# A hybrid mixer block on one core: bias rows replicated with the 128 rows outermost, result tiles reserved when a projection begins, and another weight order

## The chip, the core and the metric

The kernel runs on one core of a Trainium2 chip. The core has five engines that work at the same time: TensorE (PE, matrix products; its weight loads are PEld), VectorE (DVE), ScalarE (ACT), GpSimd (POOL) and SyncE (SP, which here only issues DMAs). Each engine runs its own instructions strictly in the order in which they were written and waits on semaphores for the others. Sixteen DMA engines move data between the chip's memory and the on-chip buffer. The metric is the device time of one execution in microseconds (us); lower is better.

## What is computed

One transformer-like block on 512 tokens of width 1024. The normalised input is multiplied by a wide matrix `w_in`, the product is split over four mixers, their outputs are multiplied by `w_out`, added to the input and normalised:

```python
h = _rmsnorm(x, norm_g[l])
p_fox, p_ssm, p_nsa, p_mem = _split(h @ w_in[l], [FOX_COLS, SSM_COLS, NSA_COLS, MEM_COLS])
mem_kv = _rmsnorm(mem, mem_norm_g[l]) @ w_mem_kv[l]
o = jnp.concatenate([
    _fox_mixer(p_fox, fox_f_bias[l]),
    _ssd_mixer(p_ssm, conv_w[l], conv_b[l], dt_bias[l], a_log[l], d_skip[l], norm_g[l]),
    _nsa_mixer(p_nsa, cmp_pe[l], cmp_w1[l], cmp_w2[l], rel_bias_table),
    _mem_mixer(p_mem, mem_kv),
], axis=-1)
x = x + o @ w_out[l]
return _rmsnorm(x, final_norm_g)
```

Fox is causal attention with forget gates (8 heads); ssd, called ssm in the kernel, a state-space scan in 4 chunks of 128 tokens; nsa compressed, selected and window attention (8 heads); mem attention to 256 memory tokens (4 heads). The nsa mixer adds a bias to each score that depends only on the distance of query and key and on the head (`rel_table[_t5_bucket(dist)]`).

## The kernel before

**Weights.** All matrices lie in memory as tiles of 128 x 1024 float32 (512 KB), one after the other in the order of the table `ORDER`. A tile takes three steps, in this order: SP loads it into one of three `raw` buffers; ACT rounds it to a short format (`wh`, function `split`); POOL subtracts to get the rest (`wl`). The matrix product is then taken as three products (`wh` with `hh`, `wh` with `hl`, `wl` with `hh`, where `hh` and `hl` are the same two parts of the input), so that a column block of 128 outputs (a "projection", `tile_a`) is 24 matmuls into a PSUM tile `pj`. There are three `wh` and three `wl` buffers too: a tile can be split when the third tile before it has been multiplied, and a `raw` buffer is free for the next load when POOL has made its `wl`. In this text T1, T2, ... are the tiles of `ORDER` from the eighth entry on, where the projections begin. `fq`, `fk`, `fg` are queries, keys and gates of fox; `kc` and `vc` keys and values for nsa's compression; `mv`, `mk`, `mq` belong to mem; `xb`, `z` to ssm; `wo` to the output product (`po`).

**Order of the work.** A planner in the kernel (`Clock`, `Sched`, `Pipe`) runs while the program is written. It keeps an estimated time for each engine and decides, step by step, whether the next matmuls are a step of one of the mixers (`fox`, `mem`, `nsa`, `ssm`, the compression `cmp`, the ssm preparation `pre`; the first `ACTIVE` entries of `PIPES`) or a piece of three matmuls of the next projection. `DF, DM, DN, DS` are how many steps each mixer may have in flight, `RF, RM, RN, RS` how many buffer slots are kept free for its later steps. `gs` and `bs` are counters of two pools of tiles; `TAKES` says what a projection takes of them. On the chip nothing of the planner is left: the engines run the written order.

A step of fox (`s1` to `s4`) is: scores on PE (`pS`), the mask and the negative row minimum on DVE (`pF`, `nm`), exponentials on ACT, reciprocal on DVE (`rs`), scaling, transposes on PE (`pT`), a copy out of PSUM (`pt`, on DVE or ACT), the product with the values on PE (`pO`). When `fq` is done, ACT and DVE make the tiles `L` (4 instructions) and then ACT makes `M` (4 instructions). `pre` builds the tiles `bd` and `cgs` on DVE. The compression multiplies `kc` and `vc`, spread out in `xst`, by weights `w1` (4 x 512 KB, loaded by SP when it begins): the matmuls `pcm`.

**The bias rows.** `rel_bias` computes 8 rows (one per head) of 656 biases (`prv`) and writes them to memory as `rv`. `spread(j)` then copies, from memory to memory, the rows of two heads (j and j + 4) 128 times each into `rows[j]`, 2 x 128 x 656 float32 (656 KB). `bias_tile(j)` later reads `rows[j]` back, with each of the 128 partitions shifted by one element. Spreads 0 and 1 are issued on SP right behind `rv`; spreads 2 and 3 when nsa begins its first and second pair of heads. SP is also the queue of every weight load.

**The end.** The last weight tiles are `wo1`, the output product of ssm. The four chunks c of ssm run between other `po` matmuls: `pR`, `pG`, `pX`, `pB` on PE; on DVE `m` (two times pR + mask), `xdt`, `xde`, two times `m` x `pG`; exponentials on ACT; then `pst` and `pY` on PE, where `pY` needs `m`, and from chunk 1 on `ce` and the state `prev` of the chunk before, which DVE makes.

Of the kernel before, what the change touches and what calls it, by code (L numbers as in the profile page):

```python
# [21 lines left out]
RVW = 656  # L22
WARM = 12
NL = 3
DF, DM, DN, DS = 5, 3, 5, 3
BACKLOG = 3000
RAW, RING = 3, 3
PIPES = "fox", "cmp", "mem", "pre", "ssm", "nsa"
LAST = 1
ACTIVE = 4  # L30

RF, RM, RN, RS = 4, 3, 2, 7

SOON, LATER, WIDE = 500, 1500, 3500

TAKES = {"fq": (2, 1), "fk": (2, 1), "fg": (1, 0), "nq": (2, 0), "ng": (1, 0), "z": (1, 0), "mq": (2, 0), "mg": (1, 0),
         "mk": (1, 0), "ks": (0, 4), "kw": (0, 4), "kc": (1, 1), "vc": (1, 1), "xb": (2, 0), "mv": (4, 0),
         "rel": (2, 0), "wo0": (5, 4), "wo1": (5, 4), "wo2": (5, 4), "wo3": (5, 4)}
# [1 line left out]
FOX, SSM, NSA, MEM = 0, 2056, 3600, 5416  # L40

ORDER = (
# [10 lines left out]
)  # L53
# [304 lines left out]
def block_kernel(ctx, tc, I, out):  # L358
    nc = tc.nc
    clock = Clock()  # L360
    V, A, P, T, Q = (Engine(e, n, clock) for e, n in (
        (nc.vector, "DVE"), (nc.scalar, "ACT"), (nc.gpsimd, "POOL"), (nc.tensor, "PE"), (nc.sync, "SP")))
# [6 lines left out]
    gs, bs = Store(NG), Store(NB)  # L369
# [5 lines left out]
    def B4(name, shape, dt=FT):  # L375
        bs.take()
        return sb.tile(shape, dt, name=name, tag="b4", bufs=NB)
# [10 lines left out]
    def PS(name):  # L388
        t = ps.tile([128, 512], FT, name=name, tag="ps", bufs=8)
        clock.bank(t.name)  # L390
        return t
# [13 lines left out]
    def unring(name, t):  # L405
        left = rings[name]
        left[0] += 1
        left[1].append(max(clock.used[t.name].values()))
        left[1].sort()
# [31 lines left out]
    def get(key):  # L441
        i = state["next"]
        assert ORDER[i] == key, (ORDER[i], key)
        state["next"] += 1
        split(i + 1)
        ahead()
        return wh.pop(i), wl.pop(i)

    def done(pair):
        unring("wh", pair[0])  # L450
        unring("wl", pair[1])
# [65 lines left out]
    def three(out_, a, b, first, last, n):  # L517
        pairs = ((a[0], b[0]), (a[0], b[1]), (a[1], b[0]))
        for i, (x, y) in enumerate(pairs):
            T.matmul(out_, x, y, start=first and i == 0, stop=last and i == 2)  # L520
# [123 lines left out]
    def memory(whole=False):  # L644

        while side and side[0]:
            if next(side[0], 1):
                side[0] = None
            if not whole:
                break  # L650
# [10 lines left out]
    def tile_a(key, sink, h=None, width=512):  # L661
        h_, l_ = get(key)
        if h:
            memory(True)
        hi, lo = h if h else (hh, hl)
        yield max(clock.ready([h_, l_, *hi, *lo]), clock.free_banks(1))
        p = PS("pj")
        for k in range(KT):
            cs = slice(k * 128, (k + 1) * 128)
            three(p[:, :width], (h_[:, cs], l_[:, cs]), (hi[k], lo[k]), k == 0, k == KT - 1, width)  # L670
            if k < KT - 1:
                yield 0.0
        done((h_, l_))
        sink(p[:, :width], key)
        if key == KEYS_A[-1]:
            gs.drop(16)
# [166 lines left out]
    def out_last(t):  # L843
# [16 lines left out]

    adders = {
        "fq": lambda k: tile_a(k, s_fq),
        "fk": lambda k: tile_a(k, s_fk),
        "fg": lambda k: tile_a(k, s_gate),
        "nq": lambda k: tile_a(k, s_q),
        "ng": lambda k: tile_a(k, s_gate),
# [160 lines left out]
    rows = [dr.tile([2, 128, RVW], FT, name=f"rows{j}") for j in range(4)]  # L1027
# [16 lines left out]
    def rel_bias():  # L1044
        sbv = G("rvs", FT, 512), G("rvt", FT, 512)
        for i in range(2):
            p = PS("prv")
            cs = slice(i * 328, (i + 1) * 328)
            T.matmul(p[:8, :328], tb, oneh[:, cs], start=True, stop=True)
            A.activation(sbv[i][:8, :328], p[:8, :328], AF.Copy, scale=-1.0)  # L1050
            Q.dma_start(out=rv[:, cs], in_=sbv[i][:8, :328])
        yield 0
        gs.drop(2)
        bs.drop()
        spread(0)
        spread(1)

    def spread(j):
        src = rv[j:j + 1, :]
        Q.dma_start(out=rows[j], in_=bass.AP(tensor=src.tensor, offset=src.offset, ap=[[4 * RVW, 2], [0, 128], [1, RVW]]))  # L1060

    def bias_tile(j):
        t = B4("bt", [128, 2, BTW])
# [8 lines left out]
    def alloc_kx():  # L1072
        if kx:
            return
        kx.extend([B4(f"k{x}{a}", [128, 1056], FR) for a in range(2)] for x in "hl")
        for a in range(2):
            P.memset(kx[1][a][64 - 64 * a:128 - 64 * a].bitcast(FT), 0.0)
            V.memset(kx[0][a][:, 512:544].bitcast(FT), 0.0)
            x = slice(64 * a, 64 * a + 64)
            V.memset(kx[1][a][x, 512:544].bitcast(FT), 0.0)  # L1080
# [83 lines left out]
    def nsa():  # L1164
        st, bts = {}, {}

        def s1(s):
            j, b, a = s
            if b == 0 and a == 0:
                if j == 0:  # L1170
                    bts[0] = bias_tile(0)
                if j < 3:
                    bts[j + 1] = bias_tile(j + 1)
                if j < 2:
                    spread(j + 2)
# [169 lines left out]
    pre = []  # L1345
# [304 lines left out]
    made = {"fox": fox, "cmp": compress, "mem": mem, "nsa": nsa, "ssm": ssm, "pre": prep}  # L1650
    bg.run([made[n]() for n in PIPES])
    while bg.todo:
# [113 lines left out]
```

## Time and profile before

| | us |
|---|---|
| median of 3 runs | 570.41 (570.08 to 571.86) |
| the profiled execution, its own time | 571.07 |
| its span, first to last instruction | 568.9 |
| PE busy in the span | 540.7 (95%) |
| PEld, DVE, ACT, POOL busy | 449.8, 332.1, 317.6, 236.4 |
| mean granted clock of PE | 0.982 of full speed |
| moved by DMA | 59.01 MB, mean 104 GB/s |

PE is busy for 95% of the span, so time goes down only where PE waits, or where it runs below full speed. The other engines are busy for about half of the time. Matmuls overlap in this profile: a matmul's own length is longer than the distance to the next one's start, and the distance is what counts for the sum.

### The profile page before, as it was taken

To read this page: it belongs to the slowest core of one execution; us is meant where nothing else is said; L and a number is where in the kernel's file an instruction comes from. 1 tells how busy PE (TensorE), PEld (TensorE's weight loads), DVE (VectorE), ACT (ScalarE), POOL (GpSimd) and SP (SyncE) were. 2 spreads that over 40 slices of the span, in tenths; PEclk is the share of its full clock that TensorE was granted. 3 is DMA by queue.
4 is the path that set the end of the run, shared out by engine and by line. 5 is a ranking of instruction groups with operands and counts; after the bars stand their busy time and mean duration, and the time that the engine had idled before them with its cause. 6 is when DMAs were issued, how large, how long until landed. Compare 5 with 4: busy or idle time off the path is not lost.

```text
span 568.9 us, 8824 instructions
## 1 busy us (share of the span) xinstructions
PE 540.7 (95%) x3237; PEld 449.8 (79%) x3237; DVE 332.1 (58%) x869; ACT 317.6 (56%) x712; POOL 236.4 (42%) x159
## 2 busy tenths in 40 slices
PE   8999999999199999999999999999999999999695
PEld 5898778777188798888888888888888888888584
DVE  2666866565057535564466546765656655666653
ACT  5756547694126655566566656656656655544333
POOL 3594514231078553334232231551533235568432
PEclk9999999999689999999999999999999999999898
DMA  7772232202723332432123211622221222123013
GB/s 286 299 264 92 103 92 75 74 15 83 240 101 99 135 112 93 138 117 75 58 103 112 74 46 67 261 74 75 74 75 38 75 74 75 38 74 112 0 39 111
DMA packets 18736, 59.01 MB, mean 104 GB/s; under 512 B 2132, under 2 KB 2404, under 8 KB 18693
## 3 DMA queue, kind: packets, MB, share of 16 engines
q1 hardware_dynamic: 18548, 58.19, 29.7%
q8 instruction: 25, 0.41, 0.3%
q10 hardware_dynamic: 144, 0.26, 0.1%
q14 instruction: 19, 0.15, 0.1%
HBM read 55.80 MB, written 4.81 MB: 107 GB/s over the span
## 4 chain that ended last, share of the span: by engine, by line
PE 79%; DVE 7%; ACT 6%; DMA 6%; issue 1%; POOL 0%; SPq 0%; POOLq 0%; DVEq 0%; ACTq 0%
PE pj L231 35%; PE po L231 15%; PE pO L231 6%; PE pb L231 6%; PE pT L231 5%; DMA raw<-in_wst 5%; PE pS L231 4%; PE pmv L231 2%; PE pW L231 1%; ACT pF L231 1%; PE pY L231 1%; DMA xt<-in_xT 1%; DVE Rl L231 1%; ACT M L231 1%; ACT wh L231 1%
## 5 line engine op out<-in xcount | busy, mean ns | idle before, releaser
L231 POOL TENSOR_TENSOR wl<-raw,wh 128x1024 fp32r<-128x1024 f32 (+1 forms) x72 | 172.2, 2396 | 282.1 <-ACT wh L231 268.6
L231 PE MATMUL pj<-hh,wh 128*128 128x512 f32 x352 | 143.4, 407 | 0.0
L231 PE MATMUL pj<-hh,wl 128*128 128x512 f32 x352 | 137.8, 392 | 0.0
L231 PE MATMUL pj<-hl,wh 128*128 128x512 f32 x352 | 137.6, 391 | 0.0
L231 ACT ACTIVATE wh<-raw 128x1024 fp32r<-128x1024 f32 (+1 forms) x72 | 74.8, 1041 | 27.8 <-DMA raw<-in_wst 23.1
L231 PEld LDWEIGHTS pj<-hh,wl 128*128 128x128 f32 x352 | 66.2, 188 | 14.8
L231 PEld LDWEIGHTS pj<-hh,wh 128*128 128x128 f32 x352 | 66.3, 188 | 13.6 <-issue 2.2
L231 PEld LDWEIGHTS pj<-hl,wh 128*128 128x128 f32 x352 | 66.5, 189 | 10.8
L231 ACT ACTIVATE pN<-pN,nm 128x128 f32<-128x128 f32 (+7 forms) x96 | 45.3, 473 | 22.9 <-DVE nm L231 22.1
L231 PE MATMUL po<-wh,oh 128*128 128x512 f32 x96 | 39.2, 409 | 0.0
L231 PE MATMUL po<-wh,ol 128*128 128x512 f32 x96 | 37.6, 392 | 0.0
L231 PE MATMUL po<-wl,oh 128*128 128x512 f32 x96 | 37.6, 391 | 0.0
L231 ACT ACTIVATE pN<-pN,rs 128x128 f32<-128x128 f32 (+3 forms) x32 | 18.0, 564 | 28.4 <-DVE rs L231 28.4
L231 DVE SCALAR_TENSOR_TENSOR sg<-sg,pj 128x512 f32<-128x512 f32 x16 | 11.0, 688 | 31.9 <-ACT sg L231 31.9
L231 DVE SCALAR_TENSOR_TENSOR xs<-cb,cwh,xs 128x512 f32<-128x512 f32 x24 | 18.0, 752 | 17.7 <-ACT xs L231 17.1
L231 DVE TENSOR_SCALAR rs<-sm 128x3 f32<-128x3 f32 x32 | 11.3, 354 | 28.7 <-ACT pN L231 28.7
L231 ACT ACTIVATE pF<-pF,nm 128x128 f32<-128x128 f32 (+3 forms) x32 | 17.7, 553 | 17.3 <-DVE nm L231 17.3
L231 DVE CUSTOM_DVE_ANT_0 pN<-pS,bt 128x128 f32<-128x128 f32 (+4 forms) x72 | 20.9, 328 | 10.2 <-PE pS L231 10.0
L231 DVE TENSOR_TENSOR acc<-acc,po 128x512 f32<-128x512 f32 (+1 forms) x33 | 21.1, 664 | 8.8 <-PE po L231 8.8
L231 PE MATMUL pO<-pt,fv 128*64 128x128 f32 x160 | 13.3, 302 | 12.0 <-ACT pt L231 12.0
L231 DVE COPY pt<-pT 128x512 f32<-128x512 f32 (+1 forms) x32 | 19.6, 618 | 7.2 <-PE pT L231 7.0
L231 PE MATMUL pT<-cst,pN 128*128 128x128 f32 x160 | 23.1, 275 | 0.0
(273 smaller groups left out, 1114.5 us busy)
## 6 DMA issues: line engine op xcount, KB each, us to landing
raw<-in_wst SPq DMA_DIRECT2D x74, 512.0 KB, 3.3
rows<-rv SPq DMA_DIRECT2D x4, 656.0 KB
bt<-rows SPq DMA_DIRECT2D x4, 528.0 KB, 4.2
xt<-in_xT SPq DMA_DIRECT2D x8, 256.0 KB, 7.0
xn<-in_xn SPq DMA_DIRECT2D x4, 512.0 KB
w<-in_w SPq DMA_DIRECT2D x4, 512.0 KB
acc<-in_xn SPq DMA_DIRECT2D x4, 512.0 KB
out<-acc SPq DMA_DIRECT2D x7, 256.0 KB, 2.2
```

Of the source, the lines that this page charges most:

```text
L231: return f(*a, **k)
```

## The change

Four things. (1) `spread` lists the dimensions of the copy in another order: the 128 repetitions outermost and the two heads inside them, for source and destination alike; the same bytes go to the same places. (2) `tile_a` takes the slots of its result from `gs` and `bs` when it begins and gives them back just before the result is written, so that the planner doesn't hand them to a mixer meanwhile; for `ks` and `kw` the key tiles `kx` are allocated (and partly zeroed) when the projection begins. (3) Numbers of the planner: depths, kept slots, the order of `PIPES`. (4) The order of the weights.

```diff
-DF, DM, DN, DS = 5, 3, 5, 3
+DF, DM, DN, DS = 6, 4, 3, 3
-PIPES = "fox", "cmp", "mem", "pre", "ssm", "nsa"
+PIPES = "fox", "pre", "cmp", "mem", "ssm", "nsa"
-RF, RM, RN, RS = 4, 3, 2, 7
+RF, RM, RN, RS = 4, 3, 2, 8
 ORDER = (
-    ("bv", 0), ("bv", 1), ("bv", 2), ("bv", 3), ("bc", 0), ("bc", 1), ("bc", 2), ("fq", 0),
-    ("fk", 0), ("fk", 2), ("vc", 0), ("fq", 3), ("fg", 0), ("fk", 1), ("fq", 1), ("fq", 2),
+    ("bv", 0), ("bv", 1), ("bv", 2), ("bv", 3), ("bc", 0), ("bc", 1), ("bc", 2), ("fq", 1),
+    ("fq", 0), ("fk", 0), ("fq", 2), ("fg", 0), ("mq", 0), ("fq", 3), ("fk", 1), ("fk", 2),
...
         hi, lo = h if h else (hh, hl)
+        if key[0] in ("ks", "kw"):
+            alloc_kx()
+        g, b = TAKES[key[0]]
+        b = 0 if key[0] in ("ks", "kw") else b
+        gs.take(g)
+        bs.take(b)
         yield max(clock.ready([h_, l_, *hi, *lo]), clock.free_banks(1))
...
         done((h_, l_))
+        gs.drop(g)
+        bs.drop(b)
         sink(p[:, :width], key)
...
     def spread(j):
         src = rv[j:j + 1, :]
-        Q.dma_start(out=rows[j], in_=bass.AP(tensor=src.tensor, offset=src.offset, ap=[[4 * RVW, 2], [0, 128], [1, RVW]]))
+        Q.dma_start(out=rows[j].rearrange("a p w -> p a w"),
+                    in_=bass.AP(tensor=src.tensor, offset=src.offset, ap=[[0, 128], [4 * RVW, 2], [1, RVW]]))
```

What this does to the order of the instructions is seen at three places.

SP's queue around the first two spreads (`rows_487`, `rows_488`), as a difference; `raw` is a weight tile, `xst` the spread-out `kc` or `vc`, `w_1502` to `w_1507` are `w1`:

```order
 L231 DMA w_496<-in_w 128x128
-L231 DMA raw<-in_wst 128x1024 x4
+L231 DMA raw<-in_wst 128x1024 x11
 L231 DMA xst<-kv 64x511
 L231 DMA xst<-kv 64x512
-L231 DMA raw<-in_wst 128x1024 x6
 L231 DMA rv<-rvs 8x328
 L231 DMA rv<-rvt 8x328
-L231 DMA rows_487<-rv 256x1x656
-L231 DMA rows_488<-rv 256x1x656
+L231 DMA rows_487<-rv 128x2x656
+L231 DMA rows_488<-rv 128x2x656
 L231 DMA raw<-in_wst 128x1024
```

Behind it both have `xst` (of `kc`); then before two weight loads and the change one, and then the four loads of `w1`. Before, ten weight tiles after `w_496` are ahead of the spreads, so the load right behind them is that of T15; in the change eleven are ahead, and the load behind them is that of T16.

ACT's queue at the first softmax of fox (`pF`), before:

```order
L231 ACTIVATE Rk<-pj 64x512 x2
L231 ACTIVATE wh<-raw 128x1024
L231 CAST ar<-pa 64x128
L231 COPY kv<-pj 128x512
L231 ACTIVATE wh<-raw 128x1024
L231 ACTIVATE pF,sm<-pF,nm 128x128 x2
```

and in the change:

```order
L231 ACTIVATE Rk<-pj 64x512 x2
L231 CAST ar<-pa 64x128
L231 ACTIVATE wh<-raw 128x1024
L231 ACTIVATE L<-pj 64x512 x2
L231 ACTIVATE M<-pj 64x512
L231 ACTIVATE M<-cst 64x512
L231 ACTIVATE M<-pj 64x512
L231 ACTIVATE M<-cst 64x512
L231 ACTIVATE wh<-raw 128x1024
L231 ACTIVATE pF,sm<-pF,nm 128x128 x2
```

The `L` and `M` of one more query block (`fq` 2) now stand ahead of the first exponentials. DVE's part of `L` stands between `cgs` and the first `pF` there.

DVE's queue at the last two ssm chunks, before:

```order
L231 TENSOR_TENSOR ol<-of,oh 128x512
L231 TENSOR_TENSOR m<-pR,umask 128x512 x2
L231 TENSOR_TENSOR xdt<-pX,dtv 128x512
L231 TENSOR_TENSOR xde<-xdt,dte 128x512
L231 TENSOR_TENSOR m<-m,pG 128x512 x2
L231 TENSOR_TENSOR acc<-acc,po 128x512 x2
L231 TENSOR_TENSOR m<-pR,umask 128x512 x2
```

and in the change:

```order
L231 TENSOR_TENSOR ol<-of,oh 128x512
L231 TENSOR_TENSOR acc<-acc,po 128x512 x2
L231 TENSOR_TENSOR m<-pR,umask 128x512 x2
L231 TENSOR_TENSOR xdt<-pX,dtv 128x512
L231 TENSOR_TENSOR xde<-xdt,dte 128x512
L231 TENSOR_TENSOR m<-m,pG 128x512 x2
L231 TENSOR_TENSOR m<-pR,umask 128x512 x2
```

The two additions of `po` to `acc` moved ahead of chunk 2. On PE the nine `po` matmuls that stood between chunk 2's `pR` to `pB` and chunk 3's `pR` now stand ahead of chunk 2's; and nine `po` of the last product stand right behind `pY`, ahead of chunk 2's `pn`.

## Rows read from the trace of the kernel before

**Rows 1.** The page: the span; PE's busy tenths in 40 slices.

```profile
span 568.9 us, 8824 instructions
...
PE   8999999999199999999999999999999999999695
```

**Rows 2.** PE's timeline: matmuls that PE waited for longest (start, length; idle before).

```profile
78.67 0.44 PE L231 MATMUL pT<-cst,pF 128*128 128x128 f32 x2 [1.42 <-ACT pF L231]
...
155.78 2.82 PE L231 MATMUL pO<-pt,fv 128*64 128x128 f32 x22 [11.97 <-ACT pt L231]
...
532.62 0.44 PE L231 MATMUL pY<-m,xdt 128*64 128x128 f32 x4 [2.93 <-DVE m L231]
535.28 0.70 PE L231 MATMUL pY<-ce,prev 128*64 128x128 f32 x4 [2.21 <-DVE prev L231]
```

**Rows 3.** ACT's timeline at the end of PE's longest wait.

```profile
154.41 1.06 ACT L231 ACTIVATE wh<-raw 128x1024 fp32r<-128x1024 f32 x1 [15.11 <-DMA raw<-in_wst]
155.37 0.84 ACT L231 COPY pt<-pT 128x256 f32<-128x256 f32 x2
```

**Rows 4.** Three pieces of the chain that ended last (start, us, what).

```profile
128.15 25.90 DMA raw<-in_wst
...
165.11 3.65 PE pcm L231 x64
...
547.31 12.29 PE po L231 x54
```

**Rows 5.** SP's timeline: its DMA issues from the first spreads on.

```profile
121.70 6.35 SPq L231 DMA_DIRECT2D rows<-rv  x2
128.15 10.18 SPq L231 DMA_DIRECT2D raw<-in_wst  x1
```

**Rows 6.** Windows: busy per engine; last three columns granted clock, DMA share, GB/s.

```profile
134.00:136.00 2.00, 2.00 (x12) 1.71 (x12) 1.49 (x4) 1.53 (x4) 0.00 (x0) 1.00 0.13 50
...
146.00:148.00 2.00, 0.00 (x0) 0.00 (x0) 0.00 (x0) 0.00 (x0) 0.00 (x0) 0.50 0.97 347
...
156.00:158.00 2.00, 2.00 (x21) 2.00 (x20) 0.00 (x0) 0.21 (x1) 2.00 (x3) 0.50 0.65 252
158.00:160.00 2.00, 2.00 (x10) 1.44 (x7) 0.00 (x0) 0.00 (x0) 2.00 (x4) 0.67 0.50 178
```

**Rows 7.** DMA issues: KB and us to landing; and SP's time (ns) for the four spreads.

```profile
raw<-in_wst SPq DMA_DIRECT2D x74, 512.0 KB, 3.3
...
L231 SPq DMA_DIRECT2D rows<-rv x4: 615/676/5605, 121.7 to 291.5; - x4
```

**Rows 8.** Timelines of PE, DVE, POOL and ACT around the first fox step.

```profile
56.14 0.39 PE L231 MATMUL pd<-cst,s 128*128 128x128 f32 x2
...
59.68 2.96 DVE L231 CAST Rl<-cr 64x512 fp32r<-64x512 f32 x2
66.10 0.86 DVE L231 CAST Rl<-cr 64x512 fp32r<-64x512 f32 x2
71.25 2.85 DVE L231 TENSOR_TENSOR bd<-ar,cst 64x512 fp32r<-64x512 f32 x1
...
68.61 4.95 POOL L231 TENSOR_TENSOR wl<-raw,wh 128x1024 fp32r<-128x1024 f32 x2 [6.26 <-ACT wh L231]
...
53.65 0.59 ACT L231 ACTIVATE M<-pj 64x512 fp32r<-64x512 f32 x1 [1.83 <-DVE L L231]
```

**Rows 9.** Timelines of PE (first row) and DVE at the last two ssm chunks.

```profile
521.82 0.62 PE L231 MATMUL pR<-bd,cgs 128*128 128x512 f32 x2
...
522.42 1.28 DVE L231 TENSOR_TENSOR m<-pR,umask 128x512 f32<-128x512 f32 x2
527.58 1.28 DVE L231 TENSOR_TENSOR acc<-acc,po 128x512 f32<-128x512 f32 x2
528.78 1.28 DVE L231 TENSOR_TENSOR m<-pR,umask 128x512 f32<-128x512 f32 x2
...
534.45 0.69 DVE L231 TENSOR_TENSOR prev<-prev,pst 128x512 f32<-128x512 f32 x1
```

12 rows, old and new, of the table ORDER are left out of this document.

## The prediction

> **What bounds the kernel now.** First the page: PE's line of busy tenths shows 9 in nearly every slice, 1 and 9 in slices 10 and 11, and less than 9 only there and in the last three [rows 1]. So PE is the bound, and what can be gained lies where it waits. Then PE's timeline, where every wait over 1 us stands with its releaser: 1.42 us at the first transposes of fox, 11.97 us at 155.78, and 2.93 and 2.21 us at `pY` of the last ssm chunk [rows 2]. The long one is the subject. It names ACT's copy `pt`; ACT's timeline shows why the copy was late: it stood behind a weight split `wh` that had waited 15.11 us for its load [rows 3]. The chain gives that load: issued at 128.15, landed 25.90 us later, at 154.05 [rows 4], where a weight load lands after 3.3 us in the median [rows 7].
>
> What held it up is seen in SP's timeline and the windows. The two spreads were issued from 121.70 on, and just behind them the load (that of T15) whose issue alone took 10.18 us [rows 5]. From 134 to 136 the DMA engines were busy for 0.13 of their time and moved 50 GB/s, while at 146 they were busy for 0.97 and moved 347 [rows 6]. 0.13 of 16 is two engines. So each spread, whose outermost dimension was the two heads, ran on two engines, one for each head, and everything issued later had its share on those two engines queue up behind. That the row is read 128 times over is not what made it slow: the two engines moved 25 GB/s each, against 347/16 = 22 in the full window.
>
> The Trainium skill ("DMA: Bandwidth & Descriptors", "Why a DMA increments its semaphore by 16 and not by 1") says that a DMA uses the largest number of engines, up to 16, that divides the slowest dimensions of both sides. By that it was 2 and becomes 16; the 0.13 agrees for the 2, and the 16 no run here shows yet for this copy.
>
> **Term 1, the spreads: -13.6 us.** Two spreads are 2 x 672 KB = 1.34 MB. From below, at the full window's 347 GB/s, they take 3.9 us; from above, if the copy gets no faster, about 26 (50 GB/s). I take 3.9, since a 512 KB load with 128 rows outermost is the nearest row in shape, and the two engines show that the repeated read doesn't slow them. What comes back is PE's 11.97 us, and the time at low clock behind it: the granted clock was 0.50 (1.2 GHz instead of 2.4) from 156 to 158 and 0.67 to 160 [rows 6] after PE had stood still, which is 2 x 0.50 + 2 x 0.33 = 1.7 us lost. Together 13.6. The later spreads (at 225 and 291) gain nothing: no wait of PE lies there.
>
> Is another load late in its place? SP's queue behind the spreads is T16, `xst`, T17 and the four `w1`, 3.3 MB, and `pcm` needs `w1`. Before, `pcm` ran at 165.11 [rows 4], that is 165.1 - 121.7 - 13.6 = 29.8 us of PE work after the spreads' issue. In the change's order 24 projection matmuls and two groups of scores with their transposes fewer lie between the bias matmuls `prv` and `pcm`: 24 x 0.228 (12.29/54 us each [rows 4]) and some 1.4 us, which leaves 23 us. The 4.6 MB with the spreads take 13.3 us at 347 GB/s and 3.3 to land: 16.6, so some 6 us are to spare.
>
> [...]
>
> **Term 2, the first fox step: +0.2 us (-1.4 to +2.5).** Before, PE waited 1.42 us for the scaled `pF`. In the change, with the same start up to `pd`'s end at 56.3 [rows 8], `fk` 0 is done at 62.8 (27 matmuls and `pa`). DVE's `L` of `fq` 0 stands where `Rl` stood, at 59.68 [rows 8], and takes 1.4; behind it come four `M` (2.45, at 0.6 each [rows 8]), a `wh` (1.04), `dte` and `decR` (0.4) and `Rk` (1.2) on ACT, to 66.1. DVE then has `Rk`/`Rl` (2.8 us), `ar` (0.3), `bd`, `cgs` (with memsets 2.1) and `L` (1.4). `bd` took 2.85 us, but POOL ran `wl` beside it [rows 8]; the pair `Rl` shows what such company costs, 2.96 against 0.86 [rows 8]. In the change POOL's next `wl` is not due there, so I take 0.7 for `bd` and keep 2.85 as the other end. `L` is done at 73.6 (75.8). Then ACT, before it may start the exponentials: four `M` and a `wh` again, to 77.1 (79.3); exponentials, reciprocal and scaling 1.5 more: 78.6 (80.9). PE comes to the transposes at 77.0 (57 projection matmuls, 8 scores, `pa` after 62.8): a wait of 1.6 (3.9) instead of 1.42. From below the wait is gone. (Lengths without a group are of the same timelines.)
>
> **Term 3, the last two ssm chunks: +1.4 us (0 to +2.5).** Between chunk 2's `pR` (521.82) and the end of `prev` (535.1) lie 13.3 us that DVE and ACT set, not PE [rows 9]; the nine `po` were in there for nothing. Now they stand ahead of chunk 2's `pR`, so this starts 9 x 0.228 = 2.05 us later. DVE's two additions (1.2 us from 527.58 to 528.78 [rows 9]) left the middle; but they now wait for those `po` to drain and push chunk 2's `m` from 0.6 to about 1.15 us behind `pR`. So 2.05 - 1.2 + 0.55 = +1.4. From below, DVE had slack that I don't see and nothing changes; from above the additions give nothing back. Behind `pY` both kernels have the same 108 `po` of the last product, without a wait of PE before, and the nine `po` ahead of `pn` only cover it.
>
> **Term 4, all else: +0.6 us (0 to +4).** Other depths and reservations move attention steps among projections from 80 to 520. PE's slices there are all 9 except in the long wait [rows 1], and the work is the same in both kernels. But the long wait let ACT, DVE and POOL catch up, and that is gone; the chain ahead of the late load already led through ACT and DVE. I take a small loss, and as the upper end two or three waits like the first fox step's. The earlier zeroing of `kx` is POOL and DVE work under projections that PE runs for 5.5 us each; uncovered it would cost about 1 us.
>
> **Sum.** 571.07 - 13.6 + 0.2 + 1.4 + 0.6 = 559.7 us for an execution like the profiled one. That one was 0.66 above the median of the runs, so 559.0. With all lower ends 571.07 - 13.6 - 1.4 - 0.66 = 555.4, with all upper ends 571.07 - 13.6 + 2.5 + 2.5 + 4 - 0.66 = 565.8.
>
> **Rivals.** (A) The forecast, 556 to 562: 0.60.
>
> (B) A smaller wait takes the long one's place, 562 to 567. Either the copy on 16 engines gets a rate between the two of rows 6, say 100 GB/s: then it takes 13.4 us, `w1` (with 9.4 us of queue and 3.3 to land) is there after 26.1 where PE needs it after 23, and the time is 559.0 + 3.1 = 562: 0.08. Or the first fox step and steps after it wait some us each, say 564: 0.12. For it speaks that the queue behind the spreads is 3.3 MB and ACT's longer list ahead of the first exponentials; against it the 6 us to spare.
>
> (C) The copy gets no faster, since one row of 5.2 KB feeds all 16 engines and the memory is the limit: the change doesn't do what it says. Then `w1` lands 25.9 + 9.4 + 3.3 = 38.6 us after the spreads' issue and PE, which is at `pcm` after 23, waits 15.6 us and loses 1.7 at low clock: 559.0 + 17.3 = 576, slower than before, since the change has less PE work between the spreads and `pcm`. It turns slower than before where the wait passes some 10 us, that is where the spreads take over 20 us (below 67 GB/s). Against it: 25 GB/s per engine on two engines, as fast as ordinary loads. 0.06 for slower, 0.04 for a rate in between that leaves about 569 to 572.
>
> (D) Better than forecast: the first step's wait goes away and chunk 3 has slack: 554.5 to 556: 0.10.
>
> So faster (by over 0.3%, 1.7 us, about what a measurement of this kernel tells from no change) 0.90, the same 0.04, slower 0.06. The range from 555.4 to 566 holds A, most of B and some of D: 0.82.
>
> **What would show it.** Right: PE's row at the `pO` of the third fox head pair has no 12 us before it, the page's slices 10 and 11 are 9 and PEclk stays 9 there; the DMA share right behind the spreads is near 1 for some 4 us, not 0.13 for 15; SP's issue of the two takes about 1.3 us (0.65 each, the usual of the four [rows 7]) instead of 6.35; no `wh` waits 15 us for its load. PE's first wait for `pF` stays between 1 and 4 us. At the end PE waits about 6.5 us in all around `pst` and `pY`, instead of 5.1. Wrong: a low DMA share behind the spreads, or `pcm` with a wait before it (B, C); waits of PE over 1 us between 160 and 520 (term 4); a first wait over 4 us (term 2). The forecast falls if PE's long wait only moves to another place.

## The result

The changed kernel takes 558.28 us (median of 4 runs, 557.51 to 558.78) against 571.0 (570.08 to 571.86) for the kernel before on the same chip: a ratio of 0.9776, 95% interval 0.9755 to 0.9798. That is faster, and 0.7 us below the forecast of 559.0. The profiled execution took 558.78 us. (On the chips of the later runs the kernel before took 572.4 to 572.9; below, such ratios are also given as us on 571.0. The ratios are those on record; they lie up to some 0.1% beside the quotients of the medians.) Of the variant "All but the spreads" one run of five took 617.16 us at a granted clock of 0.84 and is left out of its ratio.

The page of the changed kernel: span, PE's busy tenths, PE's granted clock in 40 slices.

```profile
span 557.0 us, 8823 instructions
...
PE   8999989999999999999999999999999999999695
...
PEclk9999999999999999999999999999999999999799
```

The 1 in slice 10, counted from 0 [rows 1], is gone; slice 11 stood at 9 before too. PE's timeline of the changed kernel: its waits over 0.5 us behind the start-up, and `pcm`, which has none.

```profile
78.10 0.33 PE L231 MATMUL pT<-cst,pF 128*128 128x128 f32 x1 [1.12 <-ACT pF L231]
79.20 0.33 PE L231 MATMUL pT<-cst,pF 128*128 128x128 f32 x1 [0.77 <-DVE pF L231]
...
150.52 1.75 PE L231 MATMUL pcm<-w,xp 128*64 128x128 f32 x28
...
513.65 1.10 PE L231 MATMUL pst<-xde,bt 128*128 128x256 f32 x4 [1.11 <-ACT m L231]
519.38 0.44 PE L231 MATMUL pY<-m,xdt 128*64 128x128 f32 x4 [2.71 <-DVE m L231]
521.95 0.69 PE L231 MATMUL pY<-ce,prev 128*64 128x128 f32 x4 [2.13 <-DVE prev L231]
```

The wait of 11.97 us [rows 2] has no successor. At the end there are 5.95 us of waits instead of 5.14. SP's timeline around the spreads, and what SP waited for between 120 and 150 (us in total, times, longest):

```profile
127.59 1.28 SPq L231 DMA_DIRECT2D rows<-rv  x2
128.97 0.56 SPq L231 DMA_DIRECT2D raw<-in_wst  x1
138.23 1.12 SPq L231 DMA_DIRECT2D xst<-kv  x2
139.46 0.53 SPq L231 DMA_DIRECT2D raw<-in_wst  x1
140.44 1.78 SPq L231 DMA_DIRECT2D w<-in_w  x4
...
SPq L231 <- ACT kv L231: 8.6, 1, 8.6
```

SP gets rid of both spreads in 1.28 us and of the load behind them in 0.56, where it had taken 6.35 and 10.18 [rows 5]. But `w1` is issued only at 140.44, since `xst` ahead of it waits for ACT's copy `kv`. The windows behind the spreads (last three columns: granted clock, DMA share, GB/s), and the times from issue to landing in that stretch, as medians:

```profile
128.00:130.00 2.00, 2.00 (x21) 1.59 (x21) 1.20 (x5) 0.84 (x3) 2.00 (x1) 1.00 0.45 97
130.00:132.00 2.00, 2.00 (x19) 1.74 (x16) 1.32 (x5) 0.96 (x4) 0.20 (x1) 1.00 0.45 130
132.00:134.00 2.00, 2.00 (x12) 1.67 (x12) 1.07 (x5) 1.77 (x6) 0.00 (x0) 1.00 0.71 281
134.00:136.00 2.00, 2.00 (x11) 1.60 (x10) 1.67 (x5) 1.18 (x4) 0.00 (x0) 1.00 0.86 321
...
w<-in_w SPq DMA_DIRECT2D x4, 512.0 KB, 8.6
raw<-in_wst SPq DMA_DIRECT2D x3, 512.0 KB, 8.8
rows<-rv SPq DMA_DIRECT2D x2, 656.0 KB, 7.5
```

Before, the share was 0.13 here [rows 6]. More engines than two take part now, but at a share of 0.45 for the first 4 us: the two spreads land 6.7 and 8.4 us after their issues, at 134.3 and 136.7, and the pair took about 8 us, not 3.9, with a weight load beside it from 129 on. `w1` lands 8.6 us after its issue, so from 149 on, and `pcm` begins at 150.52: almost nothing was to spare.

### The profile page after: what moved, and what is told of

It is laid out like the page before. It is cut to its first block, busy times and chain, and to the rows that moved or that the text cites. A ratio compares the mean times of both kernels' runs of the same rounds, so it can differ in the third digit from the quotient of the medians.

```text
span 557.0 us, 8823 instructions
## 1 busy us (share of the span) xinstructions
PE 540.5 (97%) x3237; PEld 449.1 (81%) x3237; DVE 325.7 (58%) x868; ACT 319.8 (57%) x713; POOL 236.6 (42%) x159
## 4 chain that ended last, share of the span: by engine, by line
PE 91%; ACT 3%; DVE 3%; issue 1%; DMA 1%; POOL 0%; POOLq 0%; SPq 0%; DVEq 0%; ACTq 0%
PE pj L231 43%; PE po L231 16%; PE pO L231 7%; PE pb L231 6%; PE pT L231 6%; PE pS L231 5%; PE pmv L231 2%; PE pW L231 2%; PE pY L231 1%; ACT m L231 1%; DMA xt<-in_xT 1%; ACT M L231 1%; PE pcm L231 1%; DVE acc L231 1%; DVE L L231 0%
## 5 line engine op out<-in xcount | busy, mean ns | idle before, releaser
L231 ACT COPY pt<-pT 128x512 f32<-128x512 f32 (+1 forms) x43 | 20.6, 492 | 8.5 <-PE pT L231 8.4
L231 DVE COPY pt<-pT 128x512 f32<-128x512 f32 (+1 forms) x29 | 18.0, 622 | 8.6 <-PE pT L231 8.4
```

The source lines that it names most:

```text
L231: return f(*a, **k)
```

## The experiments

**The spreads alone.** The kernel before with this edit only; all engines' instructions keep their order.

```diff
-        Q.dma_start(out=rows[j], in_=bass.AP(tensor=src.tensor, offset=src.offset, ap=[[4 * RVW, 2], [0, 128], [1, RVW]]))
+        Q.dma_start(out=rows[j].rearrange("a p w -> p a w"),
+                    in_=bass.AP(tensor=src.tensor, offset=src.offset, ap=[[0, 128], [4 * RVW, 2], [1, RVW]]))
```

> The kernel before, with the new dimension order of the spreads as its only edit; the order of the instructions is that of before on every engine. Theory: the spreads are the whole gain, so the time is 571.0 - 13.6 = 557.4 us (556.4 to 558.4), as fast as the changed kernel (558.3) or a little faster, with no wait of PE over 3 us and the granted clock at 1.00 from 140 on. Rival: the new weight order and depths carry part of the gain, since they set which load stands behind the spreads; then this kernel keeps a wait of some us there and takes 561 us or more.

Measured: 559.49 us against 572.87, ratio 0.9753 (0.9728 to 0.9778), 556.9 on 571.0; span 555.0 instead of 568.9. PE's timeline has three waits over 1 us behind the start-up:

```profile
78.69 0.44 PE L231 MATMUL pT<-cst,pF 128*128 128x128 f32 x2 [1.42 <-ACT pF L231]
...
518.62 0.44 PE L231 MATMUL pY<-m,xdt 128*64 128x128 f32 x4 [2.93 <-DVE m L231]
521.28 0.70 PE L231 MATMUL pY<-ce,prev 128*64 128x128 f32 x4 [2.21 <-DVE prev L231]
```

These are three of the four of [rows 2], with the same lengths; the fourth is gone with nothing in its place. So this one statement is the whole gain, and the rest of the change adds none that can be measured.

**All but the spreads.** The changed kernel with the old statement of `spread`.

> The changed kernel with the old spreads, two heads outermost. Theory: the two spreads take some 26 us on two engines, T16, xst, T17 and the four w1 land behind them, about 38.6 us after the spreads' issue; PE reaches pcm after 23, waits 15.6 us there and loses 1.7 us at low clock: 558.3 + 17.3 = 575.6 us (572 to 578), slower than before (571.0). Rival 1: the new order had already taken the loads out of the spreads' way; then about 558 to 562. Rival 2: the loss is that of the kernel before, about 12 us of wait: 570 to 572.

Measured: 577.05 us against 572.87, ratio 1.0063 (1.0033 to 1.0092), 574.6 on 571.0. PE's, SP's and POOL's timelines:

```profile
164.66 0.66 PE L231 MATMUL pcm<-w,xp 128*64 128x128 f32 x2 [13.16 <-POOL xp L231]
167.20 3.22 PE L231 MATMUL pcm<-w,xp 128*64 128x128 f32 x27 [1.88 <-POOL xp L231]
...
130.75 18.48 SPq L231 DMA_DIRECT2D raw<-in_wst  x1
149.36 1.37 SPq L231 DMA_DIRECT2D xst<-kv  x2
...
161.84 2.75 POOL L231 TENSOR_TENSOR xp<-xst,vec 128x248 f32<-128x248 f32 x4 [19.24 <-DMA xst<-kv]
```

PE waits 15.04 us at `pcm`, where 15.6 were expected. What came last was not `w1` but `xst`, which POOL must first turn into `xp`. `xst` was issued only at 149.36, behind a weight load whose issue alone took 18.48 us, and landed 12 us later. The other three parts with the old spreads make the kernel slower than before, by 0.6%, with nearly the wait of rival C but another load at its end.

**Four engines instead of two.** The kernel before, each spread as two DMAs.

```diff
-        Q.dma_start(out=rows[j], in_=bass.AP(tensor=src.tensor, offset=src.offset, ap=[[4 * RVW, 2], [0, 128], [1, RVW]]))
+        for h in range(2):
+            Q.dma_start(out=rows[j][h].rearrange("(p q) w -> p q w", p=4),
+                        in_=bass.AP(tensor=src.tensor, offset=src.offset + 4 * RVW * h, ap=[[0, 4], [0, 32], [1, RVW]]))
```

> The kernel before with each spread split into two DMAs, one for each head, whose outermost dimension is 4 (of 32 repetitions each) instead of 2 for both. Theory: the outermost dimension sets the number of engines, 4 here; at the 25 GB/s that each of the two engines moved before, the four copies run at 100 GB/s, so the DMA share behind them is near 0.25 and they take 13.4 us instead of 26.8; the load behind them lands some 13 us earlier, which is enough to take away the 12 us wait: about 557.5 us (557 to 560). Rival 1: the rate doesn't go with the number of engines, since one row of 2.6 KB feeds all: 50 GB/s and 571 us. Rival 2: the engines are not set by this dimension; then a share of 0.13 (571 us) or near 1 (557.5 us).

Measured: 557.18 us in one run, span 555.0, the same three waits as with the spreads alone. Windows, while the copies ran:

```profile
124.00:126.00 2.00, 2.00 (x16) 1.43 (x16) 1.04 (x7) 1.36 (x6) 0.00 (x0) 1.00 0.26 79
126.00:128.00 2.00, 2.00 (x21) 1.79 (x18) 1.34 (x3) 1.83 (x3) 0.57 (x1) 1.00 0.26 68
```

0.26 is four engines of 16, and this already takes the whole wait away. They moved 68 to 79 GB/s, 17 to 20 each, not the 25 each that two engines moved: a first sign that the rate doesn't grow in proportion to the engines.

**Seven kept slots for ssm.** The changed kernel with `RS = 7`, which moves nine `po` back between the last two chunks.

> The changed kernel with 7 kept slots for ssm, as before, instead of 8; this moves only the nine po back between the third and the fourth chunk's pR, and the nine of the last product back behind pn. Theory, from the alignment of the two traces: at equal PE work the changed kernel loses about 2.4 us in the last two chunks (from chunk 2's pR to the end 47.5 us against 47.1, with 9 x 0.228 us of po fewer in it), so this kernel takes 558.3 - 2.4 = 555.9 us and beats both. By the prediction's term of 1.4 us it takes 556.9. Rival: the end is bounded by PE's work and the waits only move; then 558.3.

Measured: 559.68 us against 572.87, ratio 0.9767 (0.9739 to 0.9794), 557.7 on 571.0: not to be told from the changed kernel. The wait at `pst` is gone and 2.93 and 2.22 us at `pY` are back, as before. But PE's granted clock behind these waits stayed low for longer. The windows of this kernel,

```profile
523.00:525.00 2.00, 2.00 (x22) 2.00 (x21) 0.99 (x4) 0.63 (x1) 1.26 (x4) 0.50 0.00 0
525.00:527.00 2.00, 2.00 (x13) 1.67 (x10) 1.22 (x6) 0.00 (x0) 1.10 (x3) 0.50 0.00 0
527.00:529.00 2.00, 2.00 (x6) 1.52 (x6) 0.81 (x4) 0.63 (x1) 0.85 (x3) 0.50 0.00 0
529.00:531.00 2.00, 2.00 (x7) 1.57 (x6) 0.00 (x0) 0.00 (x0) 0.48 (x1) 0.59 0.04 8
```

and of the kernel with the spreads alone, which has the same instructions there:

```profile
522.00:524.00 2.00, 2.00 (x22) 2.00 (x20) 0.78 (x3) 0.63 (x1) 1.26 (x3) 0.50 0.00 0
524.00:526.00 2.00, 2.00 (x15) 1.54 (x12) 1.48 (x6) 0.00 (x0) 0.98 (x3) 0.92 0.00 0
```

From the second `pY` wait to the end it is 558.5 - 522.51 = 36.0 us here and 555.0 - 521.28 = 33.7 there, for the same matmuls behind nearly the same waits. So some 2 us at the end hang on how long the clock stays at 0.50 (1.2 GHz) behind the same standstill, not on the order.

**Without the reservation.** The changed kernel without the lines `alloc_kx`, `take` and `drop` in `tile_a`.

> The changed kernel without the reservation of result tiles and without the early kx. The instructions of all five engines then stand in the same order with the same tiles as in the changed kernel. Theory: the reservation does nothing here, so the ratio to before is that of the changed kernel, 0.9776 (0.975 to 0.980), 558 us on a before of 571.0, with the same waits of PE (1.9 us at the first fox step, 6 us at the end); the stretch at low clock at the end may differ in length, as it did between two kernels with the same end. Rival: something that the order doesn't show (addresses, semaphores) makes a difference: outside 0.975 to 0.980, or other waits.

Measured: 558.11 us against 572.38, ratio 0.975 (0.9729 to 0.977), 556.7 on 571.0, with the same waits of PE (1.02 and 0.78 us at the first fox step; 1.11, 2.71 and 1.87 at the end). The reservation does nothing here.

**Five kept slots, with the spreads alone.** The kernel before with the new `spread` and `RS = 5`: an attempt to cover the waits of the end.

> The kernel before with the new spreads and 5 kept slots for ssm instead of 7; the second number moves only the end: 24 po instead of 9 stand between chunk 2's pR and its pst, 9 po between the pY of chunk 2 and of chunk 3, and the last product begins that much earlier. The spreads alone gave 0.9753 of before, 556.9 us on its 571.0. Theory: PE's waits at the end (2.93 and 2.21 us) are covered by these po except some 2 us at chunk 3's pY, and the stretch at low clock behind them, 1 to 3 us lost, shrinks or goes; so 552.5 us (550.5 to 554.5), a ratio of 0.964 to 0.971, faster than both kernels. Rival: the chain through DVE and ACT only moves on to chunk 3's prs and the last additions, with fewer po left to cover them: 555.5 to 558 us, a ratio of 0.973 or more.

Measured: 557.82 us against 572.38, ratio 0.9744 (0.9723 to 0.9766), 556.4 on 571.0: no faster than the spreads alone. PE's timeline at the end:

```profile
533.00 1.38 PE L231 MATMUL prs<-cst,rsr 128*128 128x128 f32 x8 [2.96 <-POOL rsr L231]
535.63 0.80 PE L231 MATMUL po<-lh,oh 128*128 128x512 f32 x1 [1.25 <-ACT oh L231]
```

The 5.14 us at `pY` are covered, and 4.21 us come back one stage later: the rival was right. No version tried beats the changed kernel by more than the measurement can tell.

**The spreads on ACT's queue.** The kernel before, old shape.

```diff
-        Q.dma_start(out=rows[j], in_=bass.AP(tensor=src.tensor, offset=src.offset, ap=[[4 * RVW, 2], [0, 128], [1, RVW]]))
+        A.real.dma_start(out=rows[j], in_=bass.AP(tensor=src.tensor, offset=src.offset, ap=[[4 * RVW, 2], [0, 128], [1, RVW]]))
```

> The kernel before with its old two-engine spreads, issued by ACT instead of SP. The copies still take some 26 us on two engines. Theory 1: a DMA waits on an engine only behind earlier DMAs of its own queue; loads of SP's queue then share the two engines with the copies, the load behind the spreads lands after some 5 us instead of 25.9, SP's issue isn't held up (10.18 us before), and the 12 us wait goes: 557 to 563 us, the upper end if ACT is held up at its second issue as SP was (5.6 us). Theory 2: each of the two engines serves all queues in the order of issue; then the load lands as late as before and the time stays at 571 us or more.

Measured: 572.49 us in one run, no gain. ACT's timeline; SP's timeline up to 160 and its longest wait on a DMA; PE's timeline; the time to landing of `w1`; and a window:

```profile
121.54 7.49 ACTq L1060 DMA_DIRECT2D rows<-rv  x2
129.14 1.06 ACT L231 ACTIVATE wh<-raw 128x1024 fp32r<-128x1024 f32 x1 [9.09 <-issue]
...
139.31 1.76 SPq L231 DMA_DIRECT2D w<-in_w  x3
...
SPq L231 <- DMA rows<-rv: 19.4, 1, 19.4
...
133.09 1.55 PE L231 MATMUL pO<-pt,fv 128*64 128x128 f32 x12 [7.57 <-ACT pt L231]
164.82 1.93 PE L231 MATMUL pcm<-w,xp 128*64 128x128 f32 x30 [2.69 <-DMA w<-in_w]
...
w<-in_w SPq DMA_DIRECT2D x4, 512.0 KB, 11.3
...
154.00:158.00 4.00, 4.00 (x20) 3.35 (x20) 1.78 (x4) 0.60 (x1) 2.59 (x5) 1.00 0.13 52
```

ACT is held up at the issue instead of SP, and PE with it for 7.57 us. SP issues three of the four `w1` from 139.31 on, but the fourth only at 160.57: before it SP waits 19.4 us until a spread has landed, though the load needs nothing of the spread (why it waits, no run shows). PE waits 2.69 us for this late load. So theory 1 failed at the issue, on both engines. Theory 2 failed at the landing: a `w1` issued at 140.26 landed 11.3 us later, at 151.6, while the copies, issued some 18 us before it, went on until about 160. ACT's queue moved 0.48 MB from 130 to 140, 0.21 from 140 to 150, when SP's loads ran beside it, and 0.40 from 150 to 160. The engines thus served both queues at once and not in the order of issue.

**Four times the spreads.** In the changed kernel three more copies behind each of the first two spreads, into tensors that nothing reads.

```diff
-        Q.dma_start(out=rows[j].rearrange("a p w -> p a w"),
-                    in_=bass.AP(tensor=src.tensor, offset=src.offset, ap=[[0, 128], [4 * RVW, 2], [1, RVW]]))
+        for d in [rows[j]] + (spare[3 * j:3 * j + 3] if j < 2 else []):
+            Q.dma_start(out=d.rearrange("a p w -> p a w"),
+                        in_=bass.AP(tensor=src.tensor, offset=src.offset, ap=[[0, 128], [4 * RVW, 2], [1, RVW]]))
```

> The changed kernel with each of the first two spreads issued four times, three of them into spare tensors that nothing reads: 6 more copies, 4.03 MB, at 347 GB/s 11.6 us more of DMA behind the first spreads. By the prediction's reckoning 6 us were to spare before pcm: a wait of 5.6 us, 564 us. The trace of the changed kernel says it otherwise: w1 was issued at 140.44, after SP had waited for ACT's copy kv, and landed at 149 to 150, when PE was at pcm at 150.52: under 2 us to spare behind w1, but DMA engines nearly idle (0.28 to 0.31) from 136 to 140; the six copies then end at 147 instead of 135.6 and delay w1 by some 6.5 us: a wait of 5 to 6.5 us and some low clock, 563.5 to 566 us. If instead the copies were limited by the memory (the pair took 8 us, not 3.9), six more take 24 us and the time is 574 us or more.

Measured: 578.51 us in one run. PE's timeline and the windows:

```profile
169.53 0.66 PE L231 MATMUL pcm<-w,xp 128*64 128x128 f32 x2 [11.83 <-DVE xp L231]
...
128.00:138.00 10.00, 10.00 (x70) 7.91 (x69) 5.91 (x20) 6.25 (x18) 2.39 (x1) 1.00 0.51 148
138.00:148.00 10.00, 10.00 (x73) 8.33 (x73) 2.85 (x6) 3.14 (x6) 2.46 (x2) 1.00 0.64 180
148.00:158.00 10.00, 9.70 (x43) 7.70 (x41) 0.62 (x2) 0.00 (x0) 0.00 (x0) 1.00 0.67 162
```

The case that the expectation named last is what came: on 16 engines these copies go at 148 to 180 GB/s, with the engines busy for 0.51 to 0.67, not at 347.

**The same bytes from another source.** As the run before this, but the six extra copies read the weights, each byte once; then with eight whole weight tiles. Both as additions to `spread` of the changed kernel:

```diff
+        for i in range(3 if j < 2 else 0):
+            k = 2 * (3 * j + i)
+            Q.dma_start(out=spare[3 * j + i].rearrange("a p w -> p a w"),
+                        in_=I["wst"][k:k + 2, :, :RVW].rearrange("a p w -> p a w"))
...
+        for i in range(4 if j < 2 else 0):
+            Q.dma_start(out=spare[4 * j + i], in_=I["wst"][4 * j + i])
```

> The changed kernel with six extra copies behind the first two spreads as in the run with each spread issued four times, of the same shape (128 x 2 pieces of 2.6 KB) and into the same spare tensors, but read from the weights, each byte once, instead of from the bias rows over and over. There the six copies and what stood beside them moved at 163 GB/s from 128 to 160 us and the time was 578.5. Theory 1, the one row that 16 engines read is what limits: these copies run near the 347 GB/s of loads, 11.6 us more DMA, and the time is about 564 us (563 to 567). Theory 2, a copy from memory to memory of this piece size is limited whatever it reads: 163 GB/s again and 576 to 580 us.

> As the run with another source, but the extra copies are eight whole weight tiles of 512 KB (4.19 MB), contiguous on both sides, so that each goes in long pieces (16 x 32 KB) instead of 256 of 2.6 KB. Theory 1 (the one row limits) and a third, that the short pieces limit: near 347 GB/s, 12 us more DMA, 564 us (563 to 567). Theory 2 (memory to memory is limited in any case): some 163 GB/s and 576 us or more.

Measured: 568.51 and 566.29 us, one run each. PE's timeline and the same windows of the first:

```profile
159.43 0.40 PE L231 MATMUL pcm<-w,xp 128*64 128x128 f32 x2 [1.32 <-DMA w<-in_w]
161.96 6.58 PE L231 MATMUL pcm<-w,xp 128*64 128x128 f32 x62 [2.12 <-DMA w<-in_w]
...
128.00:138.00 10.00, 10.00 (x69) 8.00 (x69) 5.74 (x21) 6.25 (x17) 2.39 (x1) 1.00 0.70 224
138.00:148.00 10.00, 10.00 (x78) 8.24 (x75) 2.76 (x6) 3.54 (x6) 2.45 (x2) 1.00 0.85 265
148.00:158.00 10.00, 10.00 (x45) 8.03 (x43) 1.91 (x5) 0.00 (x0) 1.32 (x2) 1.00 1.03 348
```

With the same destinations and piece sizes, 10 us come back when the source is not the bias rows. Theory 1 holds, with 1.5 us more than its range (two of the eight copies are still spreads, which may be why); with long pieces the rates are 247, 293 and 345, only a little more, so the piece size matters less than the source. The third window has mostly `w1` in it, issued from 148.90 on. Whether the limit is that the rows are read over and over, or the place in memory where `rv` lies, these runs don't separate.

## Why the prediction was right, and where not

**Term 1** (-13.6 us) was right in size and place. Alone the spreads give 571.0 x (1 - 0.9753) = 14.1 us (12.7 to 15.5), and 13.9 by the spans.

One sentence under it failed: "I take 3.9", for the two spreads at 347 GB/s. The pair took about 8 us, 1.34 MB at 168 GB/s, and the DMA share near 1 for 4 us that should have shown it was 0.45 to 0.86 for 8. The reason given for 3.9, that the repeated read doesn't slow the copy, holds for two engines at 25 GB/s each and not for 16: there the source is the limit, as the runs with another source show. A rate between the two of [rows 6] stood in rival B, at a chance of 0.08. The Trainium skill ("DMA: Bandwidth & Descriptors", "Latency and other measured facts") has copies between tensors in the chip's memory at 103 GB/s where the rows lie 4 MiB apart and at 214 with 4 KiB more between them; the 148 to 180 here lies between the two, but no run here tests the pitch of the rows. The same page's rule on the number of engines ("Why a DMA increments its semaphore by 16 and not by 1") agrees at 2 (0.13) and at 4 (0.26).

**"Some 6 us are to spare"** failed too. `pcm` came 23 us after the spreads' issue, as reckoned. But `w1` landed after about 21.5, not 16.6, and the last of the four later still: the sum counted bytes in SP's queue and left out that `xst` in it waits for ACT's `kv`, 8.6 us. Rival B was therefore nearer than its price said. What kept it away is that SP's wait and the slow copies lay beside each other: the copies were done at 136.7, SP went on at 138.23. The prediction had not seen this, so that its 3.9 did no harm was luck. With four engines, in the old order, and with 16 in both orders PE saw nothing of either.

**Term 2** (+0.2): PE waits 1.12 + 0.77 = 1.89 us at the first fox step, predicted 1.6, [rows 2] 1.42. The chain came as reckoned up to ACT: `bd` took 0.68 us (0.7), ACT began the exponentials at 76.55 (77.1). The 0.77 was not in it: DVE's scaling took 1.50 us beside POOL's `wl`, and 0.29 in the kernel before. The first scores start 0.27 us earlier than with the spreads alone (71.12 against 71.39): together +0.2.

**Term 3** (+1.4): from chunk 2's `pR` to the second `pY` wait's end it is 521.95 - 509.49 = 12.46 us, and 13.46 before (535.28 - 521.82), with 2.05 us of `po` moved out: +1.05. The waits are 5.95 us, predicted 6.5.

**Term 4** (+0.6): from 80 to 513 PE has no wait over 0.34 us. Chunk 2's `pR` begins at 509.49 with nine `po` more ahead, and at 507.81 with the spreads alone: 509.49 - 2.05 - 507.81 = -0.4 for terms 2 and 4 together, +0.8 predicted. (The prediction's reading of [rows 1] passes over slice 0, at 8, and counts slice 38, at 9, among the lower ones; nothing rests on either.)

**Not in the sum** was the low clock behind the last waits. From the second `pY` wait to the end it is 557.0 - 521.95 = 35.05 us against 568.9 - 535.28 = 33.6: +1.4. It isn't the change's: with the same order the kernel without the reservation took 556.2 - 522.05 = 34.15, and the kernel with seven slots 36.0 for an end that took 33.7 elsewhere. Summed over the spans: -13.9 - 0.4 + 1.05 + 1.4 = -11.9, which is 568.9 to 557.0, where the four terms forecast -11.4. That it came so close is partly luck: terms 2 and 4 cost 1.2 us less than forecast, and the low clock took 1.4 that the sum had nothing for.

**Rival C** had its price right: with the old spreads the new order waits 15.04 us at `pcm` (15.6 predicted) and comes out 0.63% slower than before, 574.6 us (576 predicted). Its mechanism, late loads behind the spreads, was right too, but the load that came last was `xst` and not `w1`.

## What to carry to other kernels

A DMA whose outermost dimension is 2 keeps two engines busy long after it is issued, and everything behind it on its queue, and the engine that issues it, waits for them: look for a DMA share of 1/16 or 2/16 in the windows just ahead of a long wait. Reordering the dimensions cost nothing, and in the old order four engines were already enough. When reckoning whether a later load is in time, walk its queue entry by entry, the waits of each for other engines included, and not only its bytes.

## What the runs showed of the hardware

Sixteen engines that copy two rows of 2.6 KB over and over move 148 to 180 GB/s, where copies of the same shape from the weights make the same two windows 224 and 265; with four engines it was 68 to 79, with two 50. A DMA on two engines also holds up the engine that issues the next ones: SP for 10.18 and 18.48 us, ACT for 7.49. On another queue it doesn't hold up the data in the same way: a load issued some 18 us after such copies landed 11.3 us later, before they were done. And the same standstill of PE can be followed by a shorter or longer stretch at 0.50 of the clock: 33.7 to 36.0 us for the same end of the program, which is as much as the other parts of this change could move.
